# Ten weight products split into two column halves, and block 1's attention scores issued for both heads at once

## The chip, the cores and the metric

The kernel runs on one core of a Trainium2 chip. The metric is the device time of one execution in microseconds (us), median of three timed runs; one further execution was taken by the hardware profiler.

## The reference, cut to what matters

Two two-layer blocks run in a row on 256 tokens of width 1024. Block 1: a chunked gMLP layer, a gated layer, chunked attention with 16 heads of 64, a second gated layer. Block 2: a hybrid mixer, a gated layer with an embedding gate, latent attention, a second gated layer with its embedding gate. The two parts that the change touches are the gated layers and the score step of the attentions:

```
def conv_ffn(h, w_in, conv_w, conv_b, w_down):        # block 1; block 2's conv_glu is alike
    a = h @ w_in                                       # 1024 -> 2 x 2816, h normalised
    a = causal_depthwise_conv(a, conv_w) + conv_b
    up, gate = split(a)
    return (silu(gate) * up) @ w_down

sc = einsum('bqhd,bkhd->bhqk', q, k) + bias            # scores of a head
p = softmax(sc)
o = einsum('bhqk,bkhd->bqhd', p, v)
```

Block 2's gated layers also compute an embedding e = rmsnorm(p @ w_proj) beside the layer. All norms are root-mean-square norms over 1024 features.

## The kernel before, in words

Activations lie transposed: 128 features on the partitions, 256 tokens along the row. A product of a weight tile (128 by 128) with such a tile is taken in three matmuls, because float32 operands are split into a high and a low part: high weight by high activation (xh,whi), high weight by low activation (xl,whi), low weight by high activation (xh,wlo). They are the three `mm` calls of `gemm_tile` (line 439), all through the helper at line 385, each with its own weight load. In the trace they write a tile named g. In a gated layer's down product the activations are called hh and hl.

Weights come as 399 chunks of eight tiles (512 KB) in the order of use. `_chunk` (line 406) loads a chunk on SyncE's queue, ScalarE makes the high part (whi, line 418), VectorE the low part (wlo, line 419), two chunks ahead of their use.

A norm is not applied to the activations before the product. `Norm.scale` (line 202) has TensorE sum the squares over the partitions: `Sums.total` (line 175) issues two float32 matmuls with a single moving column, each of which runs as two passes, so four passes in the trace, written to a tile s or t. VectorE turns the sums into a reciprocal root and a diagonal matrix; `Norm.spread` (line 206, `bcast` line 550) multiplies it by ones with one 256-column float32 matmul, which shows as two passes t<-dg. These are "the totals" and "the broadcast" below.

`gated_layer` (line 800) lists 352 steps; a step n is one weight tile's product, three matmuls. FFN1_PLACES and FFN2_PLACES (lines 119 and 120) say before which step a side task is put: the totals before step 13, the broadcast before step 27. In block 2 the embedding (`Embed.step`, line 301) is called behind steps 79, 127, 175 and 223 for twelve products each, behind step 255 for its own totals and behind step 287 for its broadcast. Behind the 352 steps comes the down product with 22 by 8 steps, then the next layer. The order on TensorE is the program's, step by step; VectorE and ScalarE are ordered by hand in block 1's gated layers alone.

The attention of block 1 follows ATT_ORDER (line 128), an order written out by hand for TensorE. `val` makes values, `k.i` and `q.i` (lines 755 and 761) the keys and queries of head pair i in 24 matmuls each, `s.i.e` (line 712) the scores of head e of the pair in two float32 matmuls (128 and 256 columns, 64 rows, two passes each) followed by the softmax on VectorE and ScalarE, `t.i.e` (line 733) three transposes, `pv.i` the values weighted, `oa` and `ob` the output product in two portions (line 668). Head 0 of a pair lies on partitions 0 to 63, head 1 on 64 to 127. `q.i` with an even i also loads the relative bias of four heads on GpSimd's queue (line 768). Score tiles have two buffers in PSUM. The order of block 2's latent attention is MLA_ORDER, unchanged.

Of the kernel before, what the change touches and what calls it, by code (L numbers as in the profile page):

```python
# [20 lines left out]
P = 128  # L21
S = 256
D = 1024
KD = D // P
FF = 2816
KF = FF // P
# [89 lines left out]

FFN1_PLACES = (0, 13, 27, 29, 32, 32, 37, 40, 46, (0, 4, 9, 17))
FFN2_PLACES = 0, 13, 27, 29, 32, 32, 37, 40, 44, (0, 1, 5, 11)  # L120

GMLP_ORDER = """
x.0 x.1 val.0.0 x.2 val.0.1 x.3 val.0.2 val.0.3 x.4 x.5 val.0.4 val.0.5 x.6 x.7 val.0.6 val.0.7 val.1.0 ns val.1.1
# [3 lines left out]
"""  # L127
ATT_ORDER = """
val.0.0 val.1.0 val.0.1 val.0.2 val.1.1 ns val.0.3 val.0.4 val.0.5 val.1.2 val.0.6 nb k.0 xq val.1.3 val.0.7 val.1.4
q.2 val.1.5 q.0 val.1.6 s.0.1 k.1 k.2 val.1.7 q.1 s.2.1 s.0.0 q.3 s.2.0 s.1.0 q.4 t.0.0 t.0.1 vev.0 s.1.1 k.3 pv.0  # L130
vev.1 t.1.0 s.3.1 t.2.0 t.1.1 s.3.0 k.4 pv.1 t.3.0 s.4.1 s.4.0 t.3.1 t.2.1 q.6 k.5 pv.2 t.4.1 q.5 pv.3 t.4.0 q.7 pv.4
s.5.0 k.6 s.5.1 t.5.0 s.6.0 k.7 t.5.1 s.6.1 s.7.0 pv.5 s.7.1 t.6.0 oa.0 t.6.1 t.7.0 pv.6 t.7.1 oa.2 pv.7 oa.1 ob.0
ob.1 ob.2 oa.5 ob.5 oa.3 oa.7 ob.3 oa.4 ob.4 oa.6 ob.6 ob.7
"""

MLA_ORDER = """
# [187 lines left out]
class Net:  # L324
# [111 lines left out]
        hi, lo = self.chunks[c]  # L436
        return hi[:, o * P:(o + n) * P], lo[:, o * P:(o + n) * P]

    def gemm_tile(self, X, ps, name, idx, cols, first=True, k0=0, ks=None, n=None):
        n = n or len(X)  # L440
        for k in range(*(ks or (0, n))):
            xh, xl = X[k]
            wh, wl = self.w(name, idx, k0 + k * P, cols)
            self.mm(ps, wh, xh, start=first and k == 0, stop=False)
            self.mm(ps, wh, xl, start=False, stop=False)
            self.mm(ps, wl, xh, start=False, stop=k == n - 1)

    def gemm_pair(self, X, ps, name, idx, parts, late=False, mid=None, at=0):

# [215 lines left out]
            env = dict(x=x, val=val, vev=vev, vn=vn, up=up, mix=mix, gate=gate, ns=nm.scale, nb=nm.spread)  # L665
            self.steps(GMLP_ORDER, env | self.out_steps(G, "a_w_out", (0,)))

    def out_steps(self, X, name, idx):

        out = {}  # L670

        def oa(i, k=KD - 2):
            out[i] = self.pg([P, S])
            self.gemm_tile(dict(enumerate(X)), out[i], name, idx, ((i * P, P),), ks=(0, k), n=KD)

        def ob(i, k=KD - 2):
            self.gemm_tile(X, out[i], name, idx, ((i * P, P),), ks=(k, KD))
            self.add_h(i, out[i])

        return dict(oa=oa, ob=ob)  # L680
# [22 lines left out]

        return vv, val, vev

    def head_steps(self, p, parts, vv, name, idx):

        nc = self.nc
        v, a = nc.vector, nc.scalar
        W, WT, O = {}, {}, []  # L710

        def s(i, e):
            q, k, bias = parts(i, e)
            ps = self.ps([P, 384])
            self.mm(ps[:, 0:128], q[:, 0:P], k[:, 0:P])
            self.mm(ps[:, 128:384], q[:, P:S], k)
            s_ = self.t(p, [P, 384], "s", bufs=3)
            m = self.t(p, [P, 2], "m", bufs=4)
            x = self.t(p, [P, 384], "e", bufs=3)
            l = self.t(p, [P, 2], "l", bufs=4)  # L720
            blocks = (slice(0, 128), slice(128, 384))
            for j, c in enumerate(blocks):
                v.tensor_tensor_reduce(s_[:, c], ps[:, c], bias[:, c], -1.0, 3e38, ALU.add, ALU.min, m[:, j:j + 1])
            for j, c in enumerate(blocks):
                a.activation(x[:, c], s_[:, c], AF.Exp, bias=m[:, j:j + 1], scale=-1.0, accum_out=l[:, j:j + 1])
            rl = self.t(p, [P, 2], "rl", bufs=4)
            v.reciprocal(rl, l)
            pn = self.t(p, [P, 384], "pn", bufs=4)
            v.tensor_scalar(pn[:, 0:128], x[:, 0:128], rl[:, 0:1], None, ALU.mult)
            a.activation(pn[:, 128:384], x[:, 128:384], AF.Copy, scale=rl[:, 1:2])  # L730
            W[i, e] = pn

        def t(i, e):
            WT[i, e] = self.turned(p, W[i, e], (0, 1, 2), "wt", 4)

        def pv(i):
            self.pv_heads([WT[i, e] for e in range(2)],
                          [[x[:, i * P + 64 * e:i * P + 64 * e + 64] for x in vv] for e in range(2)], O)

        return dict(s=s, t=t, pv=pv) | self.out_steps(O, name, idx)  # L740

    def attention_block1(self):
        nc, d = self.nc, self.d
        v, a = nc.vector, nc.scalar
        nm = Norm(self, self.cols("kv_norm_g", ()))
        with self.phase("att1", 16) as p:
            vv, val, vev = self.value_steps(p, nm.X, "w_kv", (), lambda hf, j: ((D + hf * 512 + j * P, P),), lambda: nm.rT)
            Xq, K, Q, B = [], {}, {}, {}

            def xq():  # L750
                bg = self.cols("b_norm_g")
                for i, h in enumerate(self.h):
                    Xq.append(self.split(h, bg[:, i:i + 1]))

            def k(i):
                ps = self.pg([P, S])
                self.gemm_tile(nm.X, ps, "w_kv", (), ((i * P, P),))
                K[i] = self.t(p, [P, S], "k", bufs=3)
                v.tensor_tensor(K[i], ps, nm.rb, ALU.mult)

            def q(i):
                ps = self.pg([P, S])
                self.gemm_tile(Xq, ps, "b_w_q", (0,), ((i * P, P),))
                Q[i] = self.t(p, [P, S], "q", bufs=3)
                v.scalar_tensor_tensor(Q[i], ps, 0.125, nm.rb, ALU.mult, ALU.mult)
                if i % 2 == 0:
                    B[i] = B[i + 1] = self.t(p, [P, 4, 384], "bias")
                    nc.gpsimd.dma_start(out=B[i], in_=d["bias"][i // 2])
                    for c in (0, 256):
                        nc.gpsimd.memset(B[i][0:64, :, c + 64:c + 128], NEG)  # L770

            def parts(i, e):
                r = slice(64 * e, 64 * e + 64)
                return Q[i][r], K[i][r], B[i][:, 2 * (i % 2) + e]

            env = dict(val=val, vev=vev, xq=xq, k=k, q=q, ns=nm.scale, nb=nm.spread)
            self.steps(ATT_ORDER, env | self.head_steps(p, parts, vv, "b_w_o", (0,)))

    def turned(self, p, w, order, tag, bufs):

# [19 lines left out]
    def gated_layer(self, nm, hid, name, l, down, stages, last, func, engines, places, extra=lambda i: None, late=lambda: None):  # L800


        scaled, conv, act = stages
        lead, ns, nb, *at, end = places

        seq = [(i, j, k) for i in range(KF) for j in range(2) for k in range(KD)]
        seq = [x for x in seq[:16] if x[2] < KD - 1] + seq[16:16 + lead] + [x for x in seq[:16] if x[2] == KD - 1] + seq[16 + lead:]
        with self.tc.manual_schedule(engines=engines):
            tile, plan = {}, {}

            def put(n, f, *j):
                plan.setdefault(n, []).append((f, j))

            put(1, lambda: self.tc.keep_in_program_order(self.nc.scalar.preload_act_table(func)))
            put(ns, nm.scale)
            put(nb, nm.spread)
            for n, f, j in zip(at, (scaled, scaled, conv, act, conv, act), (0, 1, 0, 0, 1, 1)):
                put(n, f, j)
            for i in range(3, KF):
                for n, f in zip((0, 1, 9), stages):  # L820
                    put(16 * i + n, f, i - 1)
            for n, (i, j, k) in enumerate(seq):
                for f, x in plan.get(n, ()):
                    f(*((x[0], tile[x[0]]) if x else ()))
                if i not in tile:
                    tile[i] = self.pg([P, 2, S])
                self.gemm_tile(nm.X, tile[i][:, j], name, (l,), (((j * KF + i) * P, P),), first=j == 0, ks=(k, k + 1))
                if n % 16 == 15:
                    extra(n // 16)

            ps = self.pg([P, 2, S])
            for n, (j, k) in enumerate(sorted(((j, k) for j in range(2) for k in range(KF)), key=lambda x: x[1] >= KF - 2)):
                if n in end[:3]:
                    stages[end.index(n)](KF - 1, tile[KF - 1])
                elif n == end[3]:
                    last()
                self.gemm_tile(hid.H, ps[:, j], *down, ((j * P, P),), first=j == 0, ks=(k, k + 1), n=KF)
        late()
        with self.pe_order():
            for j in range(2):  # L840
                self.add_h(j, ps[:, j])
            self.proj_residual(hid.H, *down, range(2, KD))
# [692 lines left out]
    def mla_body(self, p, nm):  # L1535
# [67 lines left out]
        def q(i, e):  # L1603
# [9 lines left out]
            lambda hf, j: tuple(((8 * hf + 2 * j + u) * P + 64, 64) for u in range(2)), lambda: R["rkT"])  # L1613
        env = dict(dn=dn, ev=ev, xkv=xkv, xq=xq, nkv=nkv, nq=nq, bkv=bkv, bq=bq, kr=kr, k=k, q=q, val=val, vev=vev,
                   ns=nm.scale, nb=nm.spread)
        heads = self.head_steps(p, lambda i, e: (Q[i, e], ks[e][i % 3], cst["causal"]), vv, "mla_w_o_2", (0,))
        self.steps(MLA_ORDER, env | heads)

    def run(self, stages=("gmlp", "f0", "att", "f1", "hyb", "g0", "mla", "g1")):
# [107 lines left out]
```

## Time and profile before

| what | before |
|---|---|
| median of three runs | 1299.81 us (1299.47 to 1301.79) |
| the profiled execution's own time | 1295.16 us |
| its span, first to last instruction | 1293.4 us |
| mean granted TensorE clock | 0.993 |
| TensorE matmuls busy, share of the span | 98% |
| TensorE weight loads busy | 94% |
| VectorE, ScalarE busy | 79%, 61% |
| share of TensorE in the chain that ended last | 94% |

The span lies 1.8 us under the execution's own time; that execution is 4.65 us faster than the median of the timed ones. A matmul's record overlaps the next one's, since they are pipelined, so busy shares say little here: the distance from one matmul's start to the next one's is read instead, from how many of them a stretch holds.

### The profile page before, as it was taken

How to read it: one execution, taken by the hardware profiler on the slowest of the kernel's cores; microseconds unless marked ns; L12 is line 12 of the kernel's file. 1: busy time of each engine (PE TensorE's matmuls, PEld its weight loads, DVE VectorE, ACT ScalarE, POOL GpSimd, SP SyncE). 2: the span in 40 equal slices, each digit the busy share in tenths (PEclk: the TensorE clock that was granted, in tenths of full speed). 3: DMA queues.
4: the chain of work that ended last, by engine and by line, in shares of the span. 5: the costliest groups of instructions: out<-in, count | busy, mean ns of one | idle time of the engine just before them, and what ended most of it. 6: DMA issues, size and time to landing. Idle time of an engine off the chain costs nothing.

```text
span 1293.4 us, 27122 instructions
## 1 busy us (share of the span) xinstructions
PE 1265.5 (98%) x10864; PEld 1210.3 (94%) x10864; DVE 1023.6 (79%) x2037; ACT 783.9 (61%) x1359; POOL 16.1 (1%) x48
## 2 busy tenths in 40 slices
PE   7999999999999999999999999999999999999997
PEld 5999999988899999999786799999999899999997
DVE  5889998566669999568975798897679878889665
ACT  6666665456666776447444466655566876565544
POOL 0000000000000000000100000000000000000000
PEclk9999999999999999999999999999999999999998
DMA  7565655555445666665350165655555335555661
GB/s 275 167 241 183 193 183 192 182 186 174 158 135 180 196 196 196 196 228 162 118 172 18 54 197 198 195 182 191 185 175 163 115 123 194 183 191 183 196 196 50
DMA packets 70398, 223.18 MB, mean 173 GB/s; under 512 B 13408, under 2 KB 15712, under 8 KB 70272
## 3 DMA queue, kind: packets, MB, share of 16 engines
q1 hardware_dynamic: 63312, 212.43, 51.1%
q10 hardware_dynamic: 6192, 5.34, 1.3%
q0 software_dynamic: 768, 3.67, 0.8%
q8 instruction: 85, 1.39, 0.4%
q14 instruction: 41, 0.34, 0.1%
HBM read 218.53 MB, written 2.88 MB: 171 GB/s over the span
## 4 chain that ended last, share of the span: by engine, by line
PE 94%; DVE 4%; ACT 1%; issue 1%; DMA 1%; SPq 0%; DVEq 0%; ACTq 0%
PE g L385 81%; PE s L385 6%; PE t L385 4%; PE o L385 2%; DVE wlo L419 1%; PE t L783 1%; DMA raw<-in_wall 1%; ACT whi L418 0%; DVE sqa L171 0%; DVE xl L497 0%; DVE b L1155 0%; DVE f L1183 0%; DVE out L260 0%; DVE GR L1181 0%; DVE h L984 0%
## 5 line engine op out<-in xcount | busy, mean ns | idle before, releaser
L385 PE MATMUL g<-xh,whi 128*128 128x256 f32 x2184 | 617.3, 283 | 1.4 <-ACT xh L496 1.4
L385 PE MATMUL g<-xl,whi 128*128 128x256 f32 x2184 | 609.3, 279 | 2.5 <-DVE xl L497 2.4
L419 DVE TENSOR_TENSOR wlo<-raw,whi 128x1024 fp32r<-128x1024 f32 (+1 forms) x400 | 487.4, 1220 | 156.4 <-ACT whi L418 153.9
L385 PE MATMUL g<-xh,wlo 128*128 128x256 f32 x2184 | 608.9, 279 | 0.3 <-DVE wlo L419 0.3
L418 ACT ACTIVATE whi<-raw 128x1024 fp32r<-128x1024 f32 (+1 forms) x400 | 422.0, 1056 | 295.6 <-PE g L385 170.5
L385 PEld LDWEIGHTS g<-xh,whi 128*128 128x128 f32 x2184 | 410.8, 188 | 7.4 <-issue 4.0
L385 PEld LDWEIGHTS g<-xl,whi 128*128 128x128 f32 x2184 | 411.4, 188 | 3.8 <-DVE xl L497 3.1
L385 PEld LDWEIGHTS g<-xh,wlo 128*128 128x128 f32 x2184 | 414.4, 190 | 0.5 <-DVE wlo L419 0.5
L385 PE MATMUL g<-hh,wlo 128*128 128x256 f32 x704 | 196.1, 279 | 0.0
L385 PE MATMUL g<-hh,whi 128*128 128x256 f32 x704 | 196.1, 278 | 0.0
L385 PE MATMUL g<-hl,whi 128*128 128x256 f32 x704 | 196.1, 278 | 0.0
L385 PEld LDWEIGHTS g<-hh,wlo 128*128 128x128 f32 x704 | 133.7, 190 | 0.0
L385 PEld LDWEIGHTS g<-hh,whi 128*128 128x128 f32 x704 | 132.2, 188 | 0.0
L385 PEld LDWEIGHTS g<-hl,whi 128*128 128x128 f32 x704 | 132.1, 188 | 0.0
L277 ACT ACTIVATE hh<-pr 128x256 fp32r<-128x256 f32 x88 | 36.0, 409 | 48.4 <-DVE pr L272 48.4
L867 ACT ACTIVATE c<-pad,vec 128x256 f32<-128x256 f32 x88 | 47.9, 592 | 23.0 <-DVE pad L856 23.0
L496 ACT ACTIVATE xh<-h,vec 128x256 fp32r<-128x256 f32 x80 | 39.1, 499 | 23.8 <-DVE h L560 20.5
L874 DVE SCALAR_TENSOR_TENSOR c<-pad,vec,c 128x256 f32<-128x256 f32 x88 | 42.7, 485 | 3.1
L497 DVE SCALAR_TENSOR_TENSOR xl<-h,vec,xh 128x256 fp32r<-128x256 f32 x80 | 37.8, 479 | 6.6 <-ACT xh L496 6.6
L872 DVE SCALAR_TENSOR_TENSOR c<-pad,vec,c 128x256 f32<-128x256 f32 x88 | 42.2, 479 | 0.0
L282 DVE TENSOR_TENSOR hl<-pr,hh 128x256 fp32r<-128x256 f32 x88 | 36.8, 419 | 3.9 <-ACT hh L277 3.9
L385 PE MATMUL g<-whi,xh 128*128 128x512 f32 x68 | 29.2, 429 | 9.5 <-ACT xh L496 9.5
(375 smaller groups left out, 1361.7 us busy)
## 6 DMA issues: line engine op xcount, KB each, us to landing
raw<-in_wall SPq DMA_DIRECT2D x398, 512.0 KB, 3.4
bias<-in_bias POOLq DMA_DIRECT2D x4, 768.0 KB, 6.9
cst_c<-in_c ACTq DMA_DIRECT2D x1, 896.0 KB, 7.0
raw<-in_wall SPq DMA_DIRECT2D x2, 256.0 KB, 4.3
h<-in_x ACTq DMA_DIRECT2D x2, 256.0 KB, 4.5
h<-in_x POOLq DMA_DIRECT2D x2, 256.0 KB, 7.6
ws<-in_ws ACTq DMA_DIRECT2D x1, 512.0 KB, 8.4
bs<-in_bs ACTq DMA_DIRECT2D x1, 512.0 KB, 8.5
```

The source lines that it names most:

```text
L277: self.net.nc.scalar.activation(self.H[-1][0], self.pr, AF.Copy)
L282: self.net.nc.vector.tensor_tensor(hl, self.pr, hh.bitcast(F32), ALU.subtract)
L385: self.nc.tensor.matmul(out, lhsT=lhsT, rhs=rhs, start=start, stop=stop, skip_group_check=True)
L418: nc.scalar.activation(hi[:, s], raw[:, s], AF.Copy)
L419: self.after(nc.vector.tensor_tensor(lo[:, s], raw[:, s], hi[:, s].bitcast(F32), ALU.subtract))
L496: self.nc.scalar.activation(xh, h, AF.Copy, scale=gain)
L497: self.nc.vector.scalar_tensor_tensor(xl, h, gain, xh.bitcast(F32), ALU.mult, ALU.subtract)
L783: self.nc.tensor.transpose(pt[:, b * P:b * P + P], w[:, s * P:s * P + P], self.cst["ident"])
L867: a.activation(c0, pad[:, j, 2:], AF.Identity, bias=self.col("f_conv_b", (l,), j * KF + i), scale=cw(2, j))
L872: v.scalar_tensor_tensor(c1, pad[:, j, 1:S + 1], cw(1, j), cc[n], ALU.mult, ALU.add)
L874: v.scalar_tensor_tensor(cc[n], pad[:, j, 0:S], cw(0, j), c1, ALU.mult, ALU.add)
```

## The change

Three edits. First, `gemm_tile` gets an argument `nudge`: at the listed k its third matmul (low weight by high activation) is issued as two, for columns 0 to 127 and 128 to 255 of the same tile. Second, such a split is asked for at ten places: in each of block 1's two gated layers at step 16; in each of block 2's two at steps 16, 226 and 258; in block 1's attention within `oa.5` and in block 2's latent attention within `oa.6`, at k = 2. Third, ATT_ORDER is rewritten: a new step `ss.i` issues the scores of both heads of pair i (head 0's first 128 columns, head 1's, then head 0's 256, head 1's) and then both softmaxes, and the sequence becomes regular: ss, a query tile, the weighted values and two transposes of the pair before, a key tile, the next ss. `soft` is the softmax half of the former `s`.

```
-FFN1_PLACES = (0, 13, 27, 29, 32, 32, 37, 40, 46, (0, 4, 9, 17))
-FFN2_PLACES = 0, 13, 27, 29, 32, 32, 37, 40, 44, (0, 1, 5, 11)
+FFN1_PLACES = (0, 13, 27, 29, 32, 32, 37, 40, 46, (0, 4, 9, 17), (16,))
+FFN2_PLACES = 0, 13, 27, 29, 32, 32, 37, 40, 44, (0, 1, 5, 11), (16, 226, 258)
...
-q.2 val.1.5 q.0 val.1.6 s.0.1 k.1 k.2 val.1.7 q.1 s.2.1 s.0.0 q.3 s.2.0 s.1.0 q.4 t.0.0 t.0.1 vev.0 s.1.1 k.3 pv.0
-vev.1 t.1.0 s.3.1 t.2.0 t.1.1 s.3.0 k.4 pv.1 t.3.0 s.4.1 s.4.0 t.3.1 t.2.1 q.6 k.5 pv.2 t.4.1 q.5 pv.3 t.4.0 q.7 pv.4
-s.5.0 k.6 s.5.1 t.5.0 s.6.0 k.7 t.5.1 s.6.1 s.7.0 pv.5 s.7.1 t.6.0 oa.0 t.6.1 t.7.0 pv.6 t.7.1 oa.2 pv.7 oa.1 ob.0
-ob.1 ob.2 oa.5 ob.5 oa.3 oa.7 ob.3 oa.4 ob.4 oa.6 ob.6 ob.7
+val.1.5 val.1.6 q.0 val.1.7 vev.1 k.1 ss.0 q.1 k.2 vev.0 ss.1 q.2 t.0.0 t.0.1 k.3 ss.2 q.3 pv.0 t.1.0 t.1.1 k.4 ss.3 q.4
+pv.1 t.2.0 t.2.1 k.5 ss.4 q.5 pv.2 t.3.0 t.3.1 k.6 ss.5 q.6 pv.3 t.4.0 t.4.1 k.7 ss.6 q.7 pv.4 t.5.0 t.5.1 ss.7 pv.5
+t.6.0 t.6.1 oa.0 pv.6 t.7.0 t.7.1 oa.2 pv.7 oa.1 ob.0 ob.1 ob.2 oa.5 ob.5 oa.3 oa.7 ob.3 oa.4 ob.4 oa.6 ob.6 ob.7
...
             self.mm(ps, wh, xh, start=first and k == 0, stop=False)
             self.mm(ps, wh, xl, start=False, stop=False)
-            self.mm(ps, wl, xh, start=False, stop=k == n - 1)
+            for c in (slice(0, P), slice(P, S)) if k in nudge else (slice(0, S),):
+                self.mm(ps[:, c], wl, xh[:, c], start=False, stop=k == n - 1)
...
+        def ss(i):
+
+            both = [(e, self.ps([P, 384]), *parts(i, e)) for e in range(2)]
+            for e, ps, q, k, bias in both:
+                self.mm(ps[:, 0:128], q[:, 0:P], k[:, 0:P])
+            for e, ps, q, k, bias in both:
+                self.mm(ps[:, 128:384], q[:, P:S], k)
+            for e, ps, q, k, bias in both:
+                soft(i, e, ps, bias)
```

## Rows read from the trace of the kernel before

**Rows 1.** The page, busy time of an engine, its share of the span, instructions.

```profile
PE 1265.5 (98%) x10864; PEld 1210.3 (94%) x10864; DVE 1023.6 (79%) x2037; ACT 783.9 (61%) x1359; POOL 16.1 (1%) x48
```

**Rows 2.** Windows of 50 us: length, PE busy (instructions), granted clock, DMA share, GB/s.

```profile
143.00:193.00 50.00, 50.00 (x427) 1.00 0.58 187
450.00:500.00 50.00, 50.00 (x444) 1.00 0.62 195
```

**Rows 3.** The chain that ended last, block 2's gated layers: start us, length us, what.

```profile
801.64 16.32 PE g L385 x144
1113.95 16.96 PE g L385 x144
```

**Rows 4.** The same chain, around totals and broadcast of the layers, and attention's end.

```profile
86.66 5.06 PE g L385 x42
92.15 177.02 PE g L385 x1503
395.46 170.27 PE g L385 x1502
582.68 8.19 PE g L385 x72
848.22 11.42 PE g L385 x96
860.07 90.45 PE g L385 x768
1075.44 18.73 PE g L385 x159
1174.19 87.07 PE g L385 x768
366.37 23.27 PE g L385 x195
```

**Rows 5.** Weight loads by form: 87 to 91.5, 390.1 to 394.8, 396 to 564 us.

```profile
L385 PEld LDWEIGHTS g<-xl,whi 128*128 128x128 f32 x13 | 2.5, 192 | 0.0
...
L385 PEld LDWEIGHTS g<-xh,wlo 128*128 128x128 f32 x14 | 2.7, 192 | 0.0
...
L385 PEld LDWEIGHTS g<-xh,wlo 128*128 128x128 f32 x323 | 60.6, 188 | 0.0
```

**Rows 6.** The chain: a run of 128-column passes and what follows; a broadcast.

```profile
42.67 0.89 PE s L385 x8
43.56 5.46 PE g L385 x48
...
91.72 0.43 PE t L385 x2
```

**Rows 7.** The chain in block 1's attention: scores (s), transposes (t L783), products (g).

```profile
309.72 0.86 PE s L385 x8
...
313.51 1.50 PE s L385 x8
...
339.06 2.74 PE g L385 x24
...
343.07 2.83 PE g L385 x24
...
350.48 0.85 PE s L385 x4
...
355.94 1.11 PE s L385 x8
...
357.87 0.85 PE s L385 x4
...
363.03 0.48 PE t L783 x3
```

**Rows 8.** Timeline at attention's end (ScalarE) and of GpSimd's queue: start, length, what.

```profile
362.01 0.51 ACT L730 ACTIVATE pn<-e,rl 128x256 f32<-128x256 f32 x1
...
321.39 0.53 POOL L768 DMA_DIRECT2D bias<-in_bias  x1 [246.26 <-DVE m L723]
```

More of the change, by code (lines that the diff above doesn't have):

```diff
@@ L437, in w, with gemm_tile @@
         return hi[:, o * P:(o + n) * P], lo[:, o * P:(o + n) * P]
-    def gemm_tile(self, X, ps, name, idx, cols, first=True, k0=0, ks=None, n=None):
+    def gemm_tile(self, X, ps, name, idx, cols, first=True, k0=0, ks=None, n=None, nudge=()):
         n = n or len(X)
@@ L666, in gmlp, with out_steps @@
             self.steps(GMLP_ORDER, env | self.out_steps(G, "a_w_out", (0,)))
-    def out_steps(self, X, name, idx):
+    def out_steps(self, X, name, idx, nudge=None):
         out = {}
@@ L673, in oa @@
             out[i] = self.pg([P, S])
-            self.gemm_tile(dict(enumerate(X)), out[i], name, idx, ((i * P, P),), ks=(0, k), n=KD)
+            self.gemm_tile(dict(enumerate(X)), out[i], name, idx, ((i * P, P),), ks=(0, k), n=KD, nudge=(2,) if i == nudge else ())
         def ob(i, k=KD - 2):
@@ L704, in value_steps, with head_steps @@
         return vv, val, vev
-    def head_steps(self, p, parts, vv, name, idx):
+    def head_steps(self, p, parts, vv, name, idx, nudge):
         nc = self.nc
@@ L716, in s, with soft @@
             self.mm(ps[:, 128:384], q[:, P:S], k)
+            soft(i, e, ps, bias)
+        def soft(i, e, ps, bias):
             s_ = self.t(p, [P, 384], "s", bufs=3)
@@ L738, in pv @@
                           [[x[:, i * P + 64 * e:i * P + 64 * e + 64] for x in vv] for e in range(2)], O)
-        return dict(s=s, t=t, pv=pv) | self.out_steps(O, name, idx)
+        return dict(s=s, ss=ss, t=t, pv=pv) | self.out_steps(O, name, idx, nudge)
     def attention_block1(self):
@@ L776, in attention_block1 @@
             env = dict(val=val, vev=vev, xq=xq, k=k, q=q, ns=nm.scale, nb=nm.spread)
-            self.steps(ATT_ORDER, env | self.head_steps(p, parts, vv, "b_w_o", (0,)))
+            self.steps(ATT_ORDER, env | self.head_steps(p, parts, vv, "b_w_o", (0,), 5))
     def turned(self, p, w, order, tag, bufs):
@@ L803, in gated_layer @@
         scaled, conv, act = stages
-        lead, ns, nb, *at, end = places
+        lead, ns, nb, *at, end, nudge = places
         seq = [(i, j, k) for i in range(KF) for j in range(2) for k in range(KD)]
@@ L826, in gated_layer @@
                     tile[i] = self.pg([P, 2, S])
-                self.gemm_tile(nm.X, tile[i][:, j], name, (l,), (((j * KF + i) * P, P),), first=j == 0, ks=(k, k + 1))
+                self.gemm_tile(nm.X, tile[i][:, j], name, (l,), (((j * KF + i) * P, P),), first=j == 0, ks=(k, k + 1),
+                               nudge=(k,) if n in nudge else ())
                 if n % 16 == 15:
@@ L1615, in mla_body @@
                    ns=nm.scale, nb=nm.spread)
-        heads = self.head_steps(p, lambda i, e: (Q[i, e], ks[e][i % 3], cst["causal"]), vv, "mla_w_o_2", (0,))
+        heads = self.head_steps(p, lambda i, e: (Q[i, e], ks[e][i % 3], cst["causal"]), vv, "mla_w_o_2", (0,), 6)
         self.steps(MLA_ORDER, env | heads)
```

## The prediction

> **What bounds the kernel now.** I read the page's busy shares first: matmuls and weight loads fill the span and nothing else comes near [rows 1]. So the question is how fast TensorE goes, not what it waits for. Windows of equal length answer it: 50 us hold 427 matmul records in the first gated layer and 444 in the second, at the same granted clock of 1.00 (the 2.4 GHz level) and the same DMA share [rows 2]. Same instructions, same clock, two speeds. The chain gives the speeds cleanly: 144 products of 256 columns take 16.32 us in one layer of block 2 and 16.96 us in the other, 113.3 and 117.8 ns each [rows 3]. I call them the fast and the slow rhythm; the difference is 4.44 ns per product.
>
> Next, where the rhythm changes. In the chain around the norms [rows 4], the stretch between totals and broadcast is slow in every gated layer (42 or 96 products at 117.8 ns, plus 0.1 us behind the totals), whatever it was before. Behind the broadcast the rhythm then stays to the next totals: 1503 products slow (177.02 us), the same layer in the other half fast (1502 in 170.27 us); 768 slow (90.45), 768 fast (87.07). The weight loads show what tells these cases apart [rows 5]: in the fast rhythm all take 188 ns; in the slow one each third takes 192 ns, on xl,whi in the stretch at 87 us (slow behind the broadcast), on xh,wlo at 390 us (fast behind it). So the rhythm is a phase that short matmuls set and a long stream keeps. The change puts a short matmul into the slow stretches.
>
> **The change, part by part.**
>
> *Splits, direct cost.* A split product issues one more matmul and one more weight load. No 128-column pass of this operand type is in the trace. The nearest row is eight float32 passes of 128 columns: 0.89 us, 0.111 each, and the 48 products behind them take 5.46 us, as 48 products of the fast rhythm do (5.44) [rows 6]. Two halves at 0.111 for one whole at 0.113: +0.11 us, ten of them **+1.1 us**; all ten lie in stretches where TensorE is the chain, so nothing hides them. Lower end the same. Upper end: a half as slow as a pass of the broadcast, 0.43 us for two [rows 6], plus 0.11 of restart as behind the totals, gives 0.54 for 0.113, +0.43 each, +4.3 in all. I take 1.1, since the column count is that of the nearer row. The wlo tile is in place already, so no load and no chunk is added.
> The Trainium skill ("TensorE: Matmul & The Clock Gate", section "Back-to-back issue gap") prices an isolated gap at columns over 2.4 plus 2.5 ns, so two halves would cost 111.7 ns against 109.2 and ten splits 0.03 us; the trace's 128-column passes cost 111 ns each, not 56, so here the row decides, and by the page's figure the sum would be 1.1 us better.
>
> *Splits, the rhythm.* What a split does to the phase is not in the trace. Nearest are breaks of 128-column passes: behind the eight passes at 42.67 us the next 48 products are fast [rows 6]; within the attention, of twelve breaks between 299 and 366 us that end in 128- or 256-column passes nine are followed by the fast rhythm and three by the slow rhythm (24 in 2.74 or 2.83 us [rows 7]). Totals, with one column, always leave slow. A half has 128 columns, so I take fast. A broadcast behind a fast stretch left fast in the one case, at 582 us (72 products in 8.19 [rows 4]). The gain, in products that turn from slow to fast (some 11 stay slow between totals and split, 3 in transition):
> - first gated layer: 28 before the broadcast, 1503 behind it [rows 4];
> - attention's output: 195 products in 23.27 us [rows 4] (the slow rhythm begins some 36 in); behind oa.5's split 150;
> - second gated layer: 28 (its 1502 are fast now and stay so);
> - block 2's first: 28, then 84 of 96 and 768 behind step 258 [rows 4];
> - block 2's second: 28, 159 [rows 4], 3 by 144 [rows 3], 4 by 12 embedding products and 96, so 763, and 84 behind step 258; the 768 at the end are fast now.
>
> That is 3436 products by 4.44 ns: **-15.3 us**. The second layer at 113.4 ns without a gap [rows 4] shows that VectorE, ScalarE and the loads can follow; they are the cover, and if they couldn't, wlo would be late next. The splits at step 226 and in oa.6 meet the fast rhythm: they cost 0.11 and gain nothing. The embedding gate behind block 2's first gated layer would be entered fast, hence left slow like the first gated layer; its chain is VectorE's there, so I take 0, at worst 150 products or 0.7 us.
>
> *Paired scores.* Scores on the chain before: eight heads alone at 0.85, two adjacent pairs on different halves of the rows at 0.86 per pair, one pair on the same half at 1.50, one at 1.11 [rows 7], 11.13 us. After: eight pairs at 0.86, 6.88. Transposes: eight groups of six behind other work (0.66 to 0.81) for 6.62 now, 6.3 after. The breaks that end in scores stay seven, those that end in transposes become seven from five at 0.02 each. Sum -4.6; at the tail both softmaxes of pair 7 start together and t.7 follows about 4.3 us later. Now head 7.1's scores begin at 357.87 and its last exponent scaling ends at 362.5, for a transpose at 363.03 [rows 7, 8]: half a microsecond of slack, which the second head's work can use up. I take 0.3 of waiting: **-4.3 us**. Ends: -4.9 with no wait, +0.5 if the interleaved passes do not overlap (eight at 1.50, as at 313.51).
> The moved steps' other work: bias loads go out in the order 0, 2, 4, 6. The third waits on GpSimd for the reductions that free its buffer, 246 us of waiting that delays nobody else in that queue [rows 8]; in the new order they come earlier and the load is needed three pairs later. SyncE's queue has the same chunks in the new order of use, 24 products each. The ss step waits for both score buffers; their last readers ran some 5 us earlier, behind a query and a key tile. Cost 0, covered by these tiles; without them PE would wait for VectorE's reductions.
>
> *Sum.* +1.1 - 15.3 - 4.3 = -18.5 us. The profiled execution has 1295.16 us (span 1293.4 and 1.8 around it), so its counterpart is 1276.7; the median of the runs lies 4.65 higher, and on it the sum gives **1281.3 us**. Should those 4.65 us be slow rhythm in the timed runs (1050 products), the splits would take them too: the low end.
>
> **The rivals.**
>
> 1. *Splits work in some layers only.* The load that is long differs between entries [rows 5], so a split may catch one phase and miss the other. Half of the 15.3: -18.5 + 7.6 gives 1289; for it speak the three slow breaks of twelve.
> 2. *Pairing gains nothing* (passes not overlapping, or softmax waits): +0.5 for -4.3, 1286.1. Against it: the pair at 0.86 [rows 7].
> 3. *Splits do nothing to the rhythm*, the totals and the broadcast alone set it, so the change doesn't do what it is made for: +1.1 - 4.3, 1296.6. The page's formula above knows only columns and clock, so by it there is one gap and this rival would be sure; the two counts at one clock [rows 2] speak against the page.
> 4. *Slower: the split leaves the slow rhythm with xl,whi long.* The place is step 16. From that phase the broadcast left slow in the first gated layer [rows 4, 5]; now it would do so in all: 1502 products of the second gated layer, 735 of block 2's first, 768 of its second turn slow, +13.3; with +1.1 - 4.3 that is +10.1, 1309.9. It decides as soon as more than 720 products turn slow (3.2 us by 4.44 ns). For it: the totals, also short, do just this. Against: they have one column, the halves 128.
>
> **How the numbers follow.** Chances: forecast 0.60, rival 1 0.14, rival 2 0.06, rival 3 0.11, rival 4 0.09. A measurement can tell about 0.2% (2.6 us) from no change. Forecast and rivals 1 and 2 are faster (0.80), rival 3 lies at -3.2 us, just beyond that bound: half and half. Faster 0.86, same 0.05, slower 0.09. The forecast's own range is 1276 to 1287: splits at +4.3 and pairing at half on the one side, pairing at -4.9 and the 4.65 us on the other. Taken to rivals 1 and 3, the range is 1276 to 1297; it leaves out rival 4.
>
> **What would show it.** Right: 50 us of any gated layer behind step 16 hold 444 records; all weight loads there take 188 ns; the stretch behind step 258 to the next totals is fast in both layers of block 2; a split and its neighbours show weight loads 111 ns apart; eight score pieces of 0.86 with eight passes each; t.7 without a wait. Wrong: 427 records behind a split (rivals 1, 3, and 4 if in the second gated layer), halves 213 ns apart, score pieces of 1.50, or TensorE waiting for ScalarE's pn. The prediction fails if the phase behind a split is not the fast one.

## The result and the profile after

The changed kernel takes 1278.4 us (median, 1276.1 to 1280.7) where the kernel before took 1300.8 beside it: a ratio of 0.9845, with a 95% interval of 0.9812 to 0.9879. Its profiled execution has 1277.48 us, of which 1275.7 are the span, at a mean granted clock of 0.994; against the profiled execution of before that is 17.7 us less.

The page's busy times of the kernel after:

```profile
PE 1247.4 (98%) x10874; PEld 1194.0 (94%) x10874; DVE 1020.1 (80%) x2037; ACT 785.8 (62%) x1359; POOL 16.2 (1%) x48
```

Against [rows 1] TensorE has ten more matmuls and ten more weight loads and is still the bound at 98%. It has not been given less to do; it goes through it at another pace. Windows of 50 us of the kernel after, behind step 16 of three gated layers (length, PE and weight loads busy with their instructions, VectorE, ScalarE, GpSimd, granted clock, DMA share, GB/s):

```profile
143.00:193.00 50.00, 50.00 (x444) 50.00 (x443) 49.36 (x85) 35.28 (x55) 0.00 (x0) 1.00 0.62 199
450.00:500.00 50.00, 50.00 (x443) 50.00 (x442) 49.29 (x85) 35.95 (x56) 0.14 (x2) 1.00 0.62 194
870.00:920.00 50.00, 50.00 (x444) 50.00 (x443) 37.35 (x65) 27.68 (x39) 0.00 (x0) 1.00 0.63 196
```

The first window answers to the 427 of [rows 2]: 444 at the same clock. VectorE is busy for 49.36 of the 50 us there, so it follows, with little left. The chain that ended last, kernel after (start us, length us, what), answers to [rows 3, 4]:

```profile
87.22 5.04 PE g L384 x43
...
92.69 171.74 PE g L384 x1509
...
385.11 170.27 PE g L384 x1502
...
838.49 11.14 PE g L384 x97
...
850.06 87.07 PE g L384 x768
...
937.47 4.35 PE g L384 x36
...
1098.65 16.32 PE g L384 x144
...
1156.93 87.07 PE g L384 x768
```

Each long stretch now has 113.3 to 113.8 ns per product (the helper stands one line higher, so L384 is L385 of before). Between totals and broadcast 43 matmuls take 5.04 us where 42 took 5.06 [rows 4]: the split has paid for itself there, no more. The 36 products behind the embedding gate's totals keep the slow rhythm (120.8 ns with the restart), as the prediction left them. The weight loads behind the first gated layer's broadcast, 93.5 to 268 us of the kernel after (by form: count, busy us, mean ns), are all alike, where the kernel before had one form at 192 ns there (last line, 93 to 268 us):

```profile
L384 PEld LDWEIGHTS g<-xh,wlo 128*128 128x128 f32 x323 | 60.6, 188 | 0.0
L384 PEld LDWEIGHTS g<-xl,whi 128*128 128x128 f32 x322 | 60.4, 188 | 0.0
...
L385 PEld LDWEIGHTS g<-xh,wlo 128*128 128x128 f32 x323 | 62.0, 192 | 0.0
```

The timeline of TensorE at the first split, kernel after (start us, length us, what); a half is of the form 128x128, and the two halves stand in one row:

```profile
88.35 0.28 PE L384 MATMUL g<-xl,whi 128*128 128x256 f32 x1
88.46 0.33 PE L384 MATMUL g<-xh,wlo 128*128 128x128 f32 x2
88.63 0.33 PE L384 MATMUL g<-xh,whi 128*128 128x256 f32 x1
88.81 0.28 PE L384 MATMUL g<-xl,whi 128*128 128x256 f32 x1
...
88.92 0.28 PE L384 MATMUL g<-xh,wlo 128*128 128x256 f32 x1
```

From the halves to the product after the next are 0.35 us; two products of the fast rhythm are 0.23. So a split costs about 0.12, and in all ten places the products behind it have the fast rhythm. Six of the ten met the slow one (those at steps 16 and 258); the other four (step 226 twice, oa.5 and oa.6) met the fast one.

In the attention, chain pieces of the kernel after: three of the paired score steps, and the longest wait of TensorE at the end.

```profile
300.88 0.86 PE s L384 x8
...
316.29 0.86 PE s L384 x8
...
340.96 0.91 PE s L384 x8
...
346.27 1.22 DVE wlo L418
347.50 0.35 DVE xl L511
347.84 0.14 issue
347.98 0.87 PE o L384 x8
```

All eight passes of a pair take 0.85 to 0.91 us in each of the seven pairs on the chain, so they overlap as the adjacent pairs of [rows 7] did. The last lines are what is new: the weighted values of pair 5 (o) start only once VectorE has made the low part (xl) of pair 4's, which stood behind a wlo. The view of waits, 283 to 380 us of the kernel after (total us, times, longest), puts 0.8 us on it, and 0.2 us on a wait at 376.5 us, in the first products of the second gated layer:

```profile
PE o L384 <- DVE xl L511: 0.8, 1, 0.8
...
PEld g L384 <- DVE xl L498: 0.2, 1, 0.2
```

Where the 17.7 us came from, stage by stage. Each stage runs from the first matmul of a totals step or a broadcast to the next such matmul, in the two profiled executions:

| stage | before | after | difference | predicted |
|---|---|---|---|---|
| first gated layer, behind its broadcast | 184.34 | 177.67 | -6.67 | -6.67 |
| attention | 106.25 | 102.05 | -4.20 | -4.86 |
| second gated layer, behind its broadcast | 177.97 | 177.72 | -0.25 | 0 |
| block 2's first layer, to step 255 | 83.76 | 83.89 | +0.13 | +0.11 |
| the same, embedding's totals to broadcast | 11.75 | 11.48 | -0.27 | -0.26 |
| the same, behind that | 90.89 | 87.50 | -3.39 | -3.41 |
| block 2's second layer, to step 255 | 87.00 | 83.89 | -3.12 | -3.15 |
| the same, embedding's totals to broadcast | 11.75 | 11.48 | -0.27 | -0.26 |
| all else (start +0.56, hybrid mixer +0.75, other parts and the end -0.94) | | | +0.37 | 0 |

### The profile page after: what moved, and what is told of

Same layout as the page of the kernel before. It is cut to its first block, busy times and chain, and to the rows that moved or that the text cites. A ratio compares the mean times of both kernels' runs of the same rounds, so it can differ in the third digit from the quotient of the medians.

```text
span 1275.7 us, 27145 instructions
## 1 busy us (share of the span) xinstructions
PE 1247.4 (98%) x10874; PEld 1194.0 (94%) x10874; DVE 1020.1 (80%) x2037; ACT 785.8 (62%) x1359; POOL 16.2 (1%) x48
## 4 chain that ended last, share of the span: by engine, by line
PE 91%; DVE 5%; DMA 2%; ACT 1%; issue 1%; ACTq 0%; SPq 0%; DVEq 0%
PE g L384 79%; PE s L384 5%; PE t L384 3%; PE o L384 2%; DVE wlo L418 1%; PE t L797 1%; DMA raw<-in_wall 1%; DMA b<-dZ 0%; ACT whi L417 0%; DMA dZ<-tm 0%; DMA dA<-b 0%; DVE xl L498 0%; DVE sqa L170 0%; DVE tm L1233 0%; DVE tm L1235 0%
## 5 line engine op out<-in xcount | busy, mean ns | idle before, releaser
L384 PE MATMUL g<-xh,whi 128*128 128x256 f32 x2184 | 614.4, 281 | 1.4 <-ACT xh L497 1.4
L384 PE MATMUL g<-xl,whi 128*128 128x256 f32 x2184 | 605.7, 277 | 2.1 <-DVE xl L498 1.9
L384 PE MATMUL g<-xh,wlo 128*128 128x256 f32 x2194 | 605.7, 277 | 0.3 <-DVE wlo L418 0.3
L384 PEld LDWEIGHTS g<-xh,whi 128*128 128x128 f32 x2184 | 410.7, 188 | 7.4 <-issue 4.3
L384 PEld LDWEIGHTS g<-xl,whi 128*128 128x128 f32 x2184 | 411.3, 188 | 3.7 <-DVE xl L498 3.0
L384 PEld LDWEIGHTS g<-xh,wlo 128*128 128x128 f32 x2194 | 412.6, 188 | 0.5 <-DVE wlo L418 0.5
L384 PE MATMUL g<-hh,wlo 128*128 128x256 f32 x704 | 194.3, 276 | 0.0
L384 PE MATMUL g<-hh,whi 128*128 128x256 f32 x704 | 194.3, 276 | 0.0
L384 PE MATMUL g<-hl,whi 128*128 128x256 f32 x704 | 194.3, 276 | 0.0
L384 PEld LDWEIGHTS g<-hl,whi 128*128 128x128 f32 x704 | 132.2, 188 | 0.0
L384 PEld LDWEIGHTS g<-hh,whi 128*128 128x128 f32 x704 | 132.2, 188 | 0.0
L384 PEld LDWEIGHTS g<-hh,wlo 128*128 128x128 f32 x704 | 132.2, 188 | 0.0
L384 PE MATMUL g<-whi,xh 128*128 128x512 f32 x68 | 29.7, 437 | 9.2 <-ACT xh L497 9.2
```

The source lines that it names most:

```text
L384: self.nc.tensor.matmul(out, lhsT=lhsT, rhs=rhs, start=start, stop=stop, skip_group_check=True)
```

## Experiments

The theory: the rhythm is a phase that short matmuls set and a stream keeps, one split sets it to the fast rhythm whatever it was, and the paired scores gain by overlap alone. The rivals: the gain is the attention's, or the splits only work where they stand or by their width.

**The splits alone.** The changed kernel with the order of before:

```
 ATT_ORDER = """
...
-val.1.5 val.1.6 q.0 val.1.7 vev.1 k.1 ss.0 q.1 k.2 vev.0 ss.1 q.2 t.0.0 t.0.1 k.3 ss.2 q.3 pv.0 t.1.0 t.1.1 k.4 ss.3 q.4
+q.2 val.1.5 q.0 val.1.6 s.0.1 k.1 k.2 val.1.7 q.1 s.2.1 s.0.0 q.3 s.2.0 s.1.0 q.4 t.0.0 t.0.1 vev.0 s.1.1 k.3 pv.0
...
```

> The ten splits with the attention order of before. Theory (a split puts the stream into the fast rhythm, whatever the phase it meets): the stages outside attention as in the changed kernel, attention's end fast behind oa.5's split; in all 14 us (13 to 15) under the kernel before, every stretch behind a split at 113.3 ns per product. Rival (the rhythm of a layer follows from how it is entered, and the new attention order is what changed that): the first gated layer stays at 117.8 ns and the sum is within 2 us of the kernel before.

Measured: 1281.49 us, ratio 0.9858 (0.9825 to 0.9890). By stages -6.67 in the first gated layer, -3.39, -3.12 and twice -0.27 in block 2, as in the changed kernel to 0.01 us, and -0.19 in the attention. The end of the second gated layer and the hybrid mixer, whose waits differ between executions, gave -1.2 and +2.1 us, so that the whole profile is 12.6 shorter, a little under the 13 to 15 expected. The splits carry the gated layers without the new order. The weight loads at the start of the attention's output (361.9 to 364.4 us) show a third form of the slow rhythm, long on xh,whi:

```profile
L385 PEld LDWEIGHTS g<-xh,whi 128*128 128x128 f32 x7 | 1.3, 192 | 0.0
```

A break at 364.6 us ends it before oa.5's split, which met the fast rhythm. The split that met this form is oa.6's, at 1043.5 us of the same execution: the six products ahead of it start 117 to 119 ns apart, the 100 behind it 113.3 ns on average.

**The pairs alone.** The new order, no split:

```
-FFN1_PLACES = (0, 13, 27, 29, 32, 32, 37, 40, 46, (0, 4, 9, 17), (16,))
-FFN2_PLACES = 0, 13, 27, 29, 32, 32, 37, 40, 44, (0, 1, 5, 11), (16, 226, 258)
+FFN1_PLACES = (0, 13, 27, 29, 32, 32, 37, 40, 46, (0, 4, 9, 17), ())
+FFN2_PLACES = 0, 13, 27, 29, 32, 32, 37, 40, 44, (0, 1, 5, 11), ()
...
-            self.steps(ATT_ORDER, env | self.head_steps(p, parts, vv, "b_w_o", (0,), 5))
+            self.steps(ATT_ORDER, env | self.head_steps(p, parts, vv, "b_w_o", (0,), None))
```

(and the same None in the latent attention)

> The new attention order without any split. Theory (totals met in the fast rhythm leave the long weight load on xl, and the broadcast then leaves slow; totals met in the slow rhythm leave it on wlo, and the broadcast leaves fast): attention itself is 3.7 us shorter, but it now ends in the fast rhythm, so the second gated layer, fast before, runs its 1502 products at 117.8 ns, +6.7; the sum is 2 to 3 us slower than before, or more if later entries turn too. Rival (a layer's rhythm does not depend on the entry): 3.7 to 4.3 us faster than before, the second layer stays at 113.3 ns.

Measured: 1297.66 us, ratio 0.9987 (0.9970 to 1.0004), no gain that can be told. The attention's stage is 3.88 us shorter, and yet the profiled execution 2.1 us longer than that of before. Its chain in the second gated layer:

```profile
386.48 5.06 PE g L384 x42
391.97 176.92 PE g L384 x1502
```

The layer that was fast in 170.27 us [rows 4] takes 6.65 more. Nothing in that layer was edited: the attention now hands over another phase. The layer's totals and broadcast pass it on, and 1502 products pay for it. The order of the attention is worth its 3.9 us in the total only where a split keeps what follows from taking over the slow rhythm. The median of 1297.7 lies between two groups of the kernel before that its further runs show below: above the one that has this layer fast, under the one that has it slow.

**No split in the second gated layer.** The changed kernel with that one left out:

```
-                             lambda: hid.last(*C.pop(KF - 1)), AF.Silu, {E.PE, E.Activation, E.DVE}, FFN1_PLACES)
+                             lambda: hid.last(*C.pop(KF - 1)), AF.Silu, {E.PE, E.Activation, E.DVE}, FFN1_PLACES[:-1] + ((),) if l else FFN1_PLACES)
```

> The changed kernel without the split in block 1's second gated layer, where the kernel before was fast anyway. Theory: the layer is entered fast now, so without its split it goes slow: 6.6 to 6.8 us slower than the changed kernel, 170 us of down-stream products at 117.8 ns. Rival (that split is idle): 0.1 us faster than the changed kernel.

Measured: 1284.17 us, ratio 0.9881 (0.9849 to 0.9913); the stage has 184.38 us against 177.72. The chain there:

```profile
385.37 176.92 PE g L384 x1502
```

So the split at step 16 of a layer that was fast in the profile of before is worth 6.66 us in the kernel that has the new order.

**The kernel before, twice more.** No edit.

> The kernel before, profiled once more, since its profiled execution (1295.2 us) lay 4.6 us under its timed runs. If executions differ in the rhythm: some stretch that was fast in the first profile is slow now, about 1000 products, and the time is near 1300. If they differ in waits or the granted clock: the same products slow, and the difference sits in the hybrid mixer or in the clock.

Measured: 1294.49 us (1292.5 to 1301.6), profiled 1293.91. Chain, and weight loads between totals and broadcast (391 to 395.6 us), of this execution:

```profile
367.18 23.28 PE g L385 x195
...
396.28 170.27 PE g L385 x1502
```

```profile
L385 PEld LDWEIGHTS g<-xh,wlo 128*128 128x128 f32 x14 | 2.7, 192 | 0.0
```

> The kernel before once more, for a profile. Its timed runs fall into two groups, 1294 to 1297 and 1300 to 1304 us. Theory (the upper group enters some layer in the other phase): an execution of the upper group has the second gated layer's 1502 products at 117.8 ns, +6.7 us; one of the lower group has them at 113.3. Rival: the rhythm is the same in both, and the difference is waits or the granted clock.

Measured: 1300.87 us (1296.9 to 1302.5), profiled 1300.64. The same two views (389.6 to 394.2 us):

```profile
366.28 22.78 PE g L385 x195
...
394.89 176.92 PE g L385 x1502
...
1176.93 90.45 PE g L385 x768
```

```profile
L385 PEld LDWEIGHTS g<-xl,whi 128*128 128x128 f32 x13 | 2.5, 192 | 0.0
```

One program, two executions, 6.7 us apart, and the second gated layer's 6.65 us are that difference. The lines also show what decides. Where the attention's output was in the slow rhythm (195 products in 23.28), the loads between totals and broadcast are long on xh,wlo and the broadcast leaves fast; where it was in the fast rhythm (22.78), they are long on xl,whi and the broadcast leaves slow. (Both times hold a few breaks besides the products. Ahead of a break at 371.2 us in the first execution and 370.3 in the second, the output is fast in both; behind it, slow in one and fast in the other.) The four profiles that have no split, these two, that of before and the pairs alone, hold 24 totals with a broadcast inside gated layers, the norm's and the embedding's: all 24 go by this rule. Block 2's halves change places in the same way: the 768 products at the end of its second layer take 90.45 here and 87.07 in [rows 4]. The 19 runs of the kernel before beside the first experiments fall into two groups, nine at 1294.2 to 1296.6 and ten at 1299.0 to 1304.4. They are not the whole spread: one of the eleven runs of before beside the last two experiments took 1288.1 us, and without a profile what was faster in it is not known.

**A split at other columns.** 32 and 224 instead of 128 and 128:

```
-            for c in (slice(0, P), slice(P, S)) if k in nudge else (slice(0, S),):
+            for c in (slice(0, 32), slice(32, S)) if k in nudge else (slice(0, S),):
```

> The changed kernel with its ten splits at column 32 instead of 128 (32 and 224). Theory (one more weight load between two long passes resets the phase, whatever the columns): within 1 us of the changed kernel, every stretch behind a split at 113.3 ns. Rival (the width of the short pass decides, and narrow ones leave the slow rhythm as the one-column totals do): the gated layers at 117.8 ns, 15 to 25 us slower than the changed kernel.

Measured: 1277.96 us, ratio 0.9827 (0.9801 to 0.9853); every gated layer as in the changed kernel. The timeline at its first split:

```profile
88.61 0.38 PE L384 MATMUL g<-xh,wlo 128*128 128x32 f32 x2
88.83 0.29 PE L384 MATMUL g<-xh,whi 128*128 128x256 f32 x1
88.96 0.28 PE L384 MATMUL g<-xl,whi 128*128 128x256 f32 x1
```

Again 0.35 us from the halves to the product after the next. Neither the effect of a split nor, to 0.02 us, its cost depends on which of the two cuts is made.

**A split later.** Behind the broadcast, at step 60, in block 1's gated layers:

```
-FFN1_PLACES = (0, 13, 27, 29, 32, 32, 37, 40, 46, (0, 4, 9, 17), (16,))
+FFN1_PLACES = (0, 13, 27, 29, 32, 32, 37, 40, 46, (0, 4, 9, 17), (60,))
```

> The changed kernel with the split of block 1's two gated layers at step 60, behind the broadcast, instead of step 16, ahead of it. Theory (a split resets the phase wherever it stands; the place ahead of the broadcast only starts the fast rhythm earlier): 132 more products per layer at 117.8 ns, 0.6 us each, 1.2 us slower than the changed kernel in all, then fast to the end of the layer. Rival (the split works through the broadcast that follows it): both layers slow throughout, 13 us slower.

Measured: 1279.45 us, ratio 0.9837 (0.9812 to 0.9862); the first gated layer +0.56 against the changed kernel. Chain behind the two broadcasts:

```profile
91.95 172.18 PE g L384 x1509
...
384.81 170.82 PE g L384 x1503
```

That is 0.44 and 0.55 us more than after. The 99 products from the broadcast to step 60 at 4.44 ns are 0.44, and the split, which stands in this stretch now, is 0.12: 0.56 in all, as in the first layer's stage. (The first layer's piece of the chain starts one product later here, so it shows less.) Neither the totals nor the broadcast are needed for a split to work: it resets a running stream.

**Fewer splits, and two in other places.** No split at step 226 and in oa.6; new splits behind the totals of the hybrid mixer and of the last embedding gate; pv.5 moved behind t.6 so that it does not wait:

```
-FFN2_PLACES = 0, 13, 27, 29, 32, 32, 37, 40, 44, (0, 1, 5, 11), (16, 226, 258)
+FFN2_PLACES = 0, 13, 27, 29, 32, 32, 37, 40, 44, (0, 1, 5, 11), (16, 258)
...
-pv.1 t.2.0 t.2.1 k.5 ss.4 q.5 pv.2 t.3.0 t.3.1 k.6 ss.5 q.6 pv.3 t.4.0 t.4.1 k.7 ss.6 q.7 pv.4 t.5.0 t.5.1 ss.7 pv.5
-t.6.0 t.6.1 oa.0 pv.6 t.7.0 t.7.1 oa.2 pv.7 oa.1 ob.0 ob.1 ob.2 oa.5 ob.5 oa.3 oa.7 ob.3 oa.4 ob.4 oa.6 ob.6 ob.7
+pv.1 t.2.0 t.2.1 k.5 ss.4 q.5 pv.2 t.3.0 t.3.1 k.6 ss.5 q.6 pv.3 t.4.0 t.4.1 k.7 ss.6 q.7 pv.4 t.5.0 t.5.1 ss.7
+t.6.0 t.6.1 pv.5 oa.0 pv.6 t.7.0 t.7.1 oa.2 pv.7 oa.1 ob.0 ob.1 ob.2 oa.5 ob.5 oa.3 oa.7 ob.3 oa.4 ob.4 oa.6 ob.6 ob.7
...
+                           nudge=(2,) if last and mid else ())
...
+                               nudge=(2,) if (key, step) == (4, 1) else ())
...
```

(and None in place of 6 in the latent attention, as in the last experiment)

> The changed kernel without the three splits that met the fast rhythm (step 226 twice, oa.6), with two new ones where the trace is still slow (behind the hybrid mixer's totals, 141 products; behind the last embedding gate's totals, 93 products), and with pv.5 behind t.6.0 and t.6.1, since TensorE waited 0.84 us there for the one buffer of the weighted values. Theory: -0.34 for the three splits, -0.6 and -0.4 for the new stretches less 0.23, -0.6 for the wait: 1.7 us faster than the changed kernel, 1.3 to 2.2. Rival (the mixer waits for other engines behind its totals, and ScalarE's copies are late in any order): 0.3 to 0.6 us faster.

Measured: 1278.74 us, ratio 0.9832 (0.9807 to 0.9857), profiled 1277.91: no gain, a miss. Leaving out step 226 gave 0.13 us in each layer, as expected of a split's direct cost. Behind the hybrid's split the products are fast, but the five ahead of it were fast already (113 to 115 ns), so it had nothing to turn here; the mixer's two parts behind it are 0.14 and 0.25 us shorter, less than they differ between executions. The attention became 0.94 us longer. The view of TensorE's waits, 343 to 366 us:

```profile
PE g L384 <- ACT xh L510: 1.0, 1, 1.0
```

The wait has not gone, it stands before the next step: pv.5's high part is late now, and the output's products want it.

**The same wait, from the other end.** pv.4 ahead of q.7, so that VectorE makes its low part before the wlo:

```
-pv.1 t.2.0 t.2.1 k.5 ss.4 q.5 pv.2 t.3.0 t.3.1 k.6 ss.5 q.6 pv.3 t.4.0 t.4.1 k.7 ss.6 q.7 pv.4 t.5.0 t.5.1 ss.7 pv.5
+pv.1 t.2.0 t.2.1 k.5 ss.4 q.5 pv.2 t.3.0 t.3.1 k.6 ss.5 q.6 pv.3 t.4.0 t.4.1 k.7 ss.6 pv.4 q.7 t.5.0 t.5.1 ss.7 pv.5
```

> The changed kernel with one step of the attention's order moved: pv.4 stands ahead of q.7 instead of behind it, so that its low part is made before the wlo that held it up. Theory (the 0.84 us before pv.5 are a wait for the only PSUM buffer of weighted values, which pv.4's low part frees too late): the wait is gone, pv.5 follows t.5 or ss.7 without a gap, the attention stage falls by 0.8 us (0.6 to 0.9) against the changed kernel's 102.05, everything else stays, profiled execution near 1276.6. Rival (the wait is the softmax of pairs 6 and 7, which TensorE meets again a step later): the stage stays within 0.2 us and a wait of the same length stands before t.6, t.7 or oa.0.

Measured: 1276.91 us (1276.6 to 1278.0), ratio 0.9844 (0.9806 to 0.9882); profiled 1277.95. The attention's stage has 102.13 against 102.05. The chain at its end:

```profile
349.65 0.36 ACT wt L799
350.01 0.41 ACT pn L744
350.42 0.37 ACT wt L799
350.80 0.04 issue
350.84 0.86 PE o L384 x5
```

The rival held: the weighted values of pair 6 now wait for ScalarE, which copies t.6 between the exponents and scalings of pair 7. Behind the one buffer stands the softmax of the last pairs, and the wait goes round with it.

**That order, and fewer splits.** The order above, no splits at 226 and in oa.6, the hybrid's split:

```
-FFN2_PLACES = 0, 13, 27, 29, 32, 32, 37, 40, 44, (0, 1, 5, 11), (16, 226, 258)
+FFN2_PLACES = 0, 13, 27, 29, 32, 32, 37, 40, 44, (0, 1, 5, 11), (16, 258)
...
-        heads = self.head_steps(p, lambda i, e: (Q[i, e], ks[e][i % 3], cst["causal"]), vv, "mla_w_o_2", (0,), 6)
+        heads = self.head_steps(p, lambda i, e: (Q[i, e], ks[e][i % 3], cst["causal"]), vv, "mla_w_o_2", (0,), None)
...
+                               nudge=(2,) if (key, step) == (4, 1) else ())
```

> The order of the run with pv.4 earlier, and in addition: no split at step 226 in block 2's two gated layers and none in oa.6 of the latent attention, and one new split in the hybrid mixer just behind its totals. Theory (a split costs 0.115 us and does nothing where the rhythm is fast already; behind the hybrid totals it turns the next products fast, most of which the mixer's own waits take back): -0.35 for the three, -0.2 for the hybrid, -0.8 for the order, about 1276.1 in the profile, 1.3 us below the changed kernel's 1277.5; the layers behind steps 226 and 258 stay fast. Rival (the splits at 226 or in oa.6 are needed to hold the phase up to step 258 or the next layer): a stretch of 768 products or a layer's first 28 turns slow, +3.4 or more in that stage.

Measured: 1277.64 us, ratio 0.9844 (0.9810 to 0.9878); profiled 1278.35. Steps 226 gave 0.13 each again. The hybrid's split met the slow rhythm this time and turned it: the stretch to the mixer's broadcast fell by 0.14 us, and the mixer's last part rose by 0.34. But the latent attention took 0.79 us more. A window behind oa.6, in this run and then in the kernel after, and the weight loads there in this run (1038.5 to 1056 us):

```profile
1038.50:1055.50 17.00, 17.00 (x147) 17.00 (x146) 14.35 (x26) 12.78 (x23) 0.00 (x0) 1.00 0.61 199
...
1038.50:1055.50 17.00, 17.00 (x153) 17.00 (x152) 14.43 (x26) 13.14 (x23) 0.00 (x0) 1.00 0.65 203
```

```profile
L384 PEld LDWEIGHTS g<-xh,wlo 128*128 128x128 f32 x50 | 9.6, 192 | 0.0
```

The kernel after has 153 products in the same 17 us, this run 147. In the run with the moved pv.5 this stretch, also without its split, was fast (152). So a split that met the fast rhythm in one profile is not idle: in the next execution it may meet the other. The other profiles show it too: oa.6's split met the slow rhythm with the splits alone and without the second layer's split, oa.5's in three runs (32 and 224 columns, splits moved, pv.4 earlier), and each time the products behind it are fast. The splits at step 226 were not missed in either run. No version beat the changed kernel by more than the runs can tell.

## Why the prediction was right, and where its sizes were off

*What bounds the kernel* held: two rhythms at one clock, 444 against 427 products in 50 us, and every stage of a gated layer that a split turned gained its number of products by 4.44 ns, within 0.03 us (table above). Rivals 1 and 3 fall with that and with the other profiles: the eight that have splits hold 76, all 76 are followed by the fast rhythm, and 54 of them met the slow one, with the long load on xl,whi (38), xh,wlo (14) or xh,whi (2). Rival 2 falls by the attention's own stage, -3.88 with the pairs alone, though the total of that run looks like it. Rival 4 had its place right, since the totals do hand a phase through the broadcast, but a split is not a totals step: none left slow. "Totals, with one column, always leave slow" was too wide, though: behind the hybrid mixer's totals in the profile of before, 66 products go at 113 ns. The Trainium skill ("TensorE: Matmul & The Clock Gate", section "Back-to-back issue gap") gives the isolated gap by column count and clock alone, and for streams of weight load and matmul one value per column count; it states none for 256 columns and no second value. The runs show two, 113.3 and 117.8 ns, for the same instructions at a granted clock of 1.00. The Trainium skill calls its formula there that of an isolated gap, so the formula did not make rival 3 sure, as the prediction has it.

*Splits, direct cost*: +0.11 each was predicted from 128-column passes; 0.12 in the timeline, 0.13 when step 226 was left out. The size was right, the reason only in part. I took it from the columns; parts of 32 and 224 cost the same to 0.02 us. It is about the time of one more product whatever its width, which fits one more weight load's slot; that is argued, not shown apart. Nor is it shown what in a split resets the stream, the added weight load or the shorter matmuls; a mere wait of TensorE leaves now the one rhythm and now the other, as the break in the attention's output does.

*Splits, the rhythm*: -15.3 was predicted, and the gated layers gave theirs to the hundredth. The term that was mis-sized is the attention's output, 150 products and -0.67 us, -0.56 with the split's cost. From the first product behind pv.7 to the second gated layer's totals it is 23.18 us before and 22.83 after: -0.35. In the profile after (and with the splits alone) a break just ahead of oa.5's split had left the fast rhythm already, so that split turned nothing and the fast products there are the break's doing; and TensorE, being earlier, then waits 0.2 us for the low part that VectorE makes of the next layer's input, a wait that the pairs alone do not have. The embedding gate left slow cost nothing, as said: its stage has 21.00 us against 21.01.

*Paired scores*: -4.3 was predicted; the attention's stage lost 4.20 with splits, 3.85 without the output's 0.35, and 3.88 with the pairs alone. The overlap gave what was worked out (-4.6 was said; -3.88 and 0.84 of waiting make -4.7). The step that was mis-sized is the wait at the tail, 0.3 us at t.7: it was 0.84 us, and at pv.5. I had looked at what t.7 needs and not at the single buffer of the weighted values, nor at VectorE's and ScalarE's queues with two softmaxes at once. That moving the wait away only moves it to pv.6 shows that the bound on it is the softmax work, as I thought, but one pair earlier.

*The sum*: -18.5 against -17.7 between the profiled executions. *The median*: 1281.3 was said, 1278.4 came. The step behind the difference is "the second layer's 1502 are fast now and stay so". In the profile they were. In one of the two further profiles of before they are slow, and by the two groups of its runs in about half of all executions; the 4.65 us between profile and median fit that, though the timed runs themselves were not traced. The split takes them too. I had named this as the low end, 1050 products by number; it is 1502 in some runs and none in others. So the gain is 17.7 us against the lower group of before and some 24 against the upper, and the changed kernel's own runs lie within 4.5 us.

What stays open: why the same break in the attention's output leaves one rhythm in one execution and the other in the next, and what in a split resets the stream. No experiment held that phase fixed.

## What to carry over

When the busiest engine is TensorE at 98% of the span, count its instructions in equal windows of like stages: two counts at one granted clock are a gain that no busy share shows. A long stream of weight load and matmul keeps the rhythm that its last interruption left; one extra short matmul in the stream, for 0.12 us, sets it, and is worth having even where the profile at hand was fast, since another execution or an edit elsewhere may hand over another phase. An edit upstream is therefore to be judged by its own stage and not by the total: here 3.9 us gained in the attention were lost again in the 177 us of the layer behind it.

## What the runs showed of the hardware that was not expected

- Weight load and matmul streams of this shape have two stable rhythms at the same granted clock of 1.00: 113.3 ns per product with all loads at 188 ns, and 117.8 with every third load at 192. A stretch of 1502 products keeps either to its end (170.27 and 176.92 us).
- The slow rhythm comes with the long load on any of a tile's three products. Totals met in the fast rhythm leave it on xl,whi and the broadcast leaves slow; met in the slow rhythm they leave it on xh,wlo and the broadcast leaves fast, in all 24 places of four profiles inside gated layers.
- One matmul issued as two column parts, 128 and 128 or 32 and 224, leaves the fast rhythm behind it, 76 times of 76. Both cuts cost the same: 0.35 us pass from the split to the product after the next, where two products take 0.23.
- The same program can take another rhythm in the next execution, worth 6.65 us in one layer here.
